# A decoder step's query and key passes: sample columns made once, TensorE in written order, rows fetched half a step ahead

## The chip, the cores and the metric

One core of one Trainium2 chip. The metric is the device time of one execution in microseconds, the median over several runs. One execution was also taken with the hardware profiler; all rows here are from it.

## The reference, cut to what matters

One step of a small decoder trunk: a state-space layer, then one shared key and value projection, then one attention layer. There are 2048 prompt rows and 8 sample rows (one new token for each of 8 sequences with 2048 cached positions), all 1024 wide. The part around the change projects the state-space layer's output x1 twice, each time after an RMS norm with its own scale and shift:

```
qz = (norm(x1) * (1 + scale_b)  + shift_b)  @ w_in_b     # 2048 + 8 rows -> queries q, gates z
kv = (norm(x1) * (1 + scale_kv) + shift_kv) @ w_kv       # 2048 + 8 rows -> keys k, values v
scores of a sample = q_sample . cached keys            # 16 pages of 128 keys, 16 heads
weights = stick-breaking(sigmoid(scores / 8 + bias))
```

Both norms divide by the same root mean square; only scale and shift differ, for the sample rows too. Keys and values of all rows are outputs.

## The kernel before, in words

The method `phase_b1` (L1085) makes both projections. Everything is float32; a product is three matmuls of reduced precision (`hi` by `hi`, `lo` by `hi`, `hi` by `lo`), so a weight `w` is kept as `w0h`, `w0l` (slot w0) or `w1h`, `w1l` (slot w1), and the normed columns as `hi`, `lo`.

**The loop** (L1190) has 16 steps, `(ps, t)`: pass 0 (queries and gates) for eight groups of 256 prompt rows, then pass 1 (keys and values) for the same eight. Group t = 1 carries the 8 sample rows beside its 256. A step of pass 0 (step 0 to 7) runs eight `q_block`s with slot w0 and eight `z_block`s with slot w1, 24 matmuls each. A step of pass 1 (step 8 to 15) runs eight `k_block`s, each followed by the two transposes (`k_rows`) of the key block before it, and two `v_block`s of 48 wide matmuls each (three for t = 1).

**The columns of the next step** are made within a step, in three parts. `norm_rows` (L1031) loads 256 rows of x1 as two tiles `x` (L1038; two buffers), has ACT take the sum of their squares (L1039), DVE a root by Newton steps (L90 to L95) and a scaling (L1043). The Square's discarded output `jk` needs a buffer of the pool tag "wraw" (three buffers), through which weight halves also stream (L890, L892, L893). `norm_cols` (L1053) is a generator: each of its eight pulls transposes 128 columns on PE into PSUM (`psC`), keeps a copy in DRAM for the second pass (`xn`, L1070 and L1071), and makes `h` (L1073, ACT), `hi` (L1074, ACT) and `lo` (L1075, POOL or DVE). In pass 1, for t > 0, `norm_again` (L1046) loads the kept transposed columns `xn`, so there are no transposes. For t = 1 a ninth pull loads the sample rows `xs` (L1079) and calls `sample_cols` (L855): Square, root, scaling (L861), eight small transposes, four DVE operations (L868 to L871).

The rows are fetched after the first block of a step (f == 0); the generator is made after block 3 (pass 0) or block 2 (pass 1) and then pulled ahead of each later block: the prompt rows' transposes stand ahead of query blocks 4 to 7 and z blocks 0 to 3, the sample rows' ahead of z block 4 or of value block 1.

**The sample keys.** Beside this, `sample_keys` (L1263) loads cached key pages (`kp`, three buffers, on SP's queue), multiplies them with the sample's query (DVE, L1275) and reduces them to scores `zs` (DVE, L1276). When a sample's scores are there, `sample_weights` makes its weights in four stages: transposes of `zs`, then of `c`, a small matmul of `E`, and transposes of `sg`, with ACT and DVE work between them. `more` pulls this stream after each query, z and key block from step 2 on and four times ahead of each value block. By the text, the four stages of sample 7, the last, all stand ahead of value block 0 of step 14, and the first stage of sample 3 right behind the key blocks of step 8.

**What sets the order.** The framework's scheduler orders each engine's instructions by a simulation of its own; the text gives only priorities. `keep_in_program_order` pins an instruction behind the one written before it on its engine; `Ordered` and `OrderedCore` apply it to whole engines, and so far only the attention phase behind this one used them. The DMAs of this phase go through SP's queue.

Of the kernel before, what the change touches and what calls it, by code (L numbers as in the profile page):

```python
# [9 lines left out]
FR = mybir.dt.float32r  # L10
# [16 lines left out]
KT = 8  # L27
# [19 lines left out]
class Ordered:  # L47


    def __init__(self, tc, engine):  # L50
        self.tc, self.engine = tc, engine
# [8 lines left out]


class OrderedCore:
    def __init__(self, tc, nc):
        self.nc = nc
        for n in ("tensor", "vector", "scalar", "gpsimd"):
            setattr(self, n, Ordered(tc, getattr(nc, n)))

    def __getattr__(self, name):
# [3 lines left out]
class Kern:  # L72
# [643 lines left out]
    def phase_a1(self):  # L716
        nc, tc, I, cp = self.nc, self.tc, self.I, self.cp
        self.W = {}
        self.uV = self.scr("uV", [NG, 8, GC, CH])
        self.uS = self.scr("uS", [D, NS])  # L720
        self.zT = self.scr("zT", [D, NC1])
        self.ygT = self.scr("ygT", [D, NC1])
        self.x1 = self.scr("x1", [NC1, D])
        self.gD = self.scr("gD", [2, 9, D])
        with ExitStack() as c1:
            self.s5c = self.pool(c1, "s5c", side="right")
            self.dmask = self.s5c.tile([64, 16], FT, name="dmask")
            nc.vector.tensor_add(self.dmask, self.idf[:64, 0:16], self.idf[:64, 32:48])
            wp = self.pool(c1, "wp", side="right")
            ep = self.pool(c1, "ep", 2, side="right")  # L730
            slots = iter(self.slots("w0"))
            self.h = [[[self.wr["w0"].tile([128, 2, 512], FR, tag=next(slots), name=f"h{cb}{g}") for _ in range(4)]
                       for g in "hl"] for cb in range(2)]
            W = lambda slot: self.split_w(wp, I["w_in_a"], 2 * D, slot * 128, 128)
            with ExitStack() as c2:
                with ExitStack() as ce:
                    early = self.pool(ce, "early")
                    early2 = self.pool(ce, "early2")
                    xp = self.pool(c2, "xp", side="right")
                    sc, sh = self.mod_tiles("a", 2)  # L740
                    with ExitStack() as c3:
                        mp = self.pool(c3, "mwp", side="right")
                        self.silu_c(early)
                        self.vectors(early)
                        b, g = self.vo["b_mod_a"], self.vo["g_pre_a"]
                        for f in range(2):
                            self.mod_finish(self.mod_wide(mp, I["w_mod_a"], f * 512, 512, 4), sh, f * 4, 4, b, None, 0)
                            self.mod_finish(self.mod_wide(mp, I["w_mod_a"], D + f * 512, 512, 4), sc, f * 4, 4, b + 8, g, 1.0)
                            if f == 0:
                                xt = self.x_block(xp, xp, 0)  # L750
                                w = [W(0), W(1)]
                    xq = self.pool(c2, "xq", side="right")
                    self.h_block(xp, 0, xt, sc, sh, range(HS))
                    xt1 = self.x_block(xp, xq, 1)
                    self.h_block(xp, 0, xt, sc, sh, range(HS, KT))
                    self.h_block(xp, 1, xt1, sc, sh, range(HS))
                    xt2 = self.x_block(xp, xp, 2)
                    self.h_block(xp, 1, xt1, sc, sh, range(HS, KT))
                    self.s5_params(early, early2)
                h23 = self.pool(c1, "h23")  # L760
                self.h += [[h23.tile([128, KT, n], FR, name=f"h{cb}{g}") for g in "hl"] for cb, n in ((2, 512), (3, 520))]
                self.h_block(xp, 2, xt2, sc, sh, range(HS))
                xt3 = self.x_block(xp, xq, 3)
                self.h_block(xp, 2, xt2, sc, sh, range(HS, KT))
                self.h_block(xp, 3, xt3, sc, sh, range(KT))
                self.kpad_zero(xp)
                xs = xp.tile([128, D], FT, tag="x", name="xs", bufs=4)[:8]
                nc.sync.dma_start(xs, I["x_sample"].rearrange("a b d -> (a b) d"))
                self.sample_cols(xp, xs, sc, sh, self.h[3][0], self.h[3][1], slice(512, 520))
            with ExitStack() as c2:  # L770
                self.sp = self.pool(c2, "sp", side="right")
                self.linears(wp, ep, w)
            with ExitStack() as c2:
                self.s5_states(self.pool(c2, "st", side="right"))
            with ExitStack() as c2:
                self.linears_tail(wp, ep, self.pool(c2, "gm", side="right"))
# [75 lines left out]
        for _ in mods:  # L852
            pass

    def sample_cols(self, pool, xs, sc, sh, hhi, hlo, cols, extra=None):  # L855

        nc = self.nc
        ss = pool.tile([8, 1], FT, tag="sss", name="sss")
        nc.scalar.activation(self.rp.tile([128, D], BF, tag="wraw", name="jk")[:8], xs, AF.Square, accum_out=ss)
        rs = self.rsqrt(pool, ss, 8, 1, "rss")  # L860
        nc.vector.tensor_scalar(xs, xs, rs, None, OP.mult)  # L861
        p = self.psC()
        for k in range(KT):
            self.tr(p[:, k * 8:(k + 1) * 8], xs[:, k * 128:(k + 1) * 128])
        pv = p[:, :64].rearrange("p (k s) -> p k s", s=8)
        for s_, b_, hi, lo in ([(sc, sh, hhi, hlo)] + ([extra] if extra else [])):
            t = pool.tile([128, KT, 8], FT, tag="sct", name="sct")
            nc.vector.tensor_mul(t, pv, s_[:, :, 1:9])  # L868
            nc.vector.tensor_add(t, t, b_[:, :, 1:9])
            nc.vector.tensor_copy(hi[:, :, cols], t)  # L870
            nc.vector.tensor_sub(lo[:, :, cols], t, hi[:, :, cols].bitcast(FT))  # L871
# [181 lines left out]
    def norm_cols(self, t, xt, mods, keep=None, kept=False):  # L1053


        nc, xp, hp = self.nc, self.xp, self.hp
        sc, sh = mods
        hi, lo = (hp[t % 2].tile([128, KT, 264], FR, tag=f"{g}{t % 2}", name=f"{g}{t % 2}") for g in ("hi", "lo"))

        def go():  # L1060
            for k in range(KT):
                if kept:
                    p = xt[k // 4][:, k % 4]
                else:
                    p = self.psC()[:, :256]
                    for i in range(2):
                        self.tr(p[:, i * 128:i * 128 + 128], xt[i][:, k * 128:(k + 1) * 128])
                if keep:
                    o = keep.tile([128, 512], FT, tag="v", name="xn")[:, :256]
                    nc.scalar.activation(o, p, AF.Copy)  # L1070
                    nc.sync.dma_start(self.xnT[k * 128:k * 128 + 128, t * 256:t * 256 + 256], o)  # L1071
                h = xp.tile([128, 256], FT, tag="h", name="h", bufs=2)
                nc.scalar.activation(h, p, AF.Identity, scale=sc[:, k, 0:1], bias=sh[:, k, 0:1])  # L1073
                nc.scalar.activation(hi[:, k, :256], h, AF.Copy)  # L1074
                (nc.gpsimd if k % 2 or kept else nc.vector).tensor_sub(lo[:, k, :256], h, hi[:, k, :256].bitcast(FT))  # L1075
                yield
            if t == 1:
                xs = xp.tile([128, D], FT, tag="x", name="xs", bufs=2)[:8]
                nc.sync.dma_start(xs, self.x1[SEQ:NC1])  # L1079
                self.sample_cols(xp, xs, sc, sh, hi, lo, slice(256, 264))  # L1080

        n = 264 if t == 1 else 256
        return go(), hi[:, :, :n], lo[:, :, :n]

    def phase_b1(self):  # L1085
        nc, tc, I, O = self.nc, self.tc, self.I, self.O

        self.kT = self.scr("kT", [NH, 2 * HD, SEQ])
        self.qT = self.scr("qT", [NH // 2, HD, 4, SEQ])
# [3 lines left out]
        with ExitStack() as c:  # L1093
            hp1 = self.pool(c, "b1h1", side="right")
            op = self.pool(c, "b1o", 2, side="right")
            sp = self.pool(c, "b1s", side="right")
            self.hp[1] = hp1
            self.sample_setup()
            units = self.sample_keys(sp)
            def fm_block(f, n, h, w):  # L1100
# [83 lines left out]
            def more():  # L1184
                done[0] += 1
                while done[1] < total * done[0] // (13 * 16):
                    done[1] += 1
                    next(units, None)

            for s, (ps, t) in enumerate(steps):  # L1190
                n = 264 if t == 1 else 256
                nxt = steps[s + 1] if s + 1 < 16 else None
                cols = iter(())
                for f in range(KT):
                    next(cols, None)
                    (k_block if ps else q_block)(f, t, n, h)
                    if s > 1:
                        more()
                    if f == 0 and nxt:
                        xt = self.norm_again(nxt[1]) if nxt[0] and nxt[1] else self.norm_rows(nxt[1])  # L1200
                    if f == (2 if ps else 3) and nxt:
                        cols, *nh = self.norm_cols(nxt[1], xt, mods[nxt[0]], None if nxt[0] else op, nxt[0] and nxt[1])
                if late:
# [10 lines left out]
                if ps == 0:  # L1214
                    for f in range(KT):
                        next(cols, None)
                        z_block(f, t, n, h)
                        if s > 1:
                            more()
# [7 lines left out]
                        v_block(i, t, h)  # L1227
                for _ in cols:
                    pass
                if nxt:  # L1230
                    h = nh
                if (ps, t) == (0, 7):
                    self.load_w("w1", I["w_kv"], 2 * D, D)
            for _ in units:
                pass


    def sample_setup(self):
# [533 lines left out]
```

## Time and profile before

| | us |
|---|---|
| median of 3 runs | 3251.82 (3247.64 to 3253.74) |
| the profiled execution | 3257.83 |
| its span on the core | 3256.1 |
| the 16 steps of `phase_b1` in it | 1083.4 to 1986.3 |

The mean granted TensorE clock of the profiled execution is 0.96 of full speed. Times in rows count from the start of the span. In rows, PE is TensorE, PEld its weight loads, DVE VectorE, ACT ScalarE, POOL GpSimd, SP SyncE; "psA<-hi,w0h" is an instruction that writes psA from hi and w0h, and a bracket behind it gives the engine's idle time ahead of it and what ended that. A row of a stretch gives its bounds, its length, then each engine's busy time with its instructions (PE, PEld, DVE, ACT, POOL), the granted TensorE clock as a share of full speed, the busy share of the DMA engines, and GB/s.

### The profile page before, as it was taken

The page shows a single profiled execution, that of the slowest core. Times are in us where ns is not written, and L with a number is a line of the kernel's source. Part 1 is how long each engine was busy: PE and PEld are TensorE (multiplying, and loading weights), DVE is VectorE, ACT ScalarE, POOL GpSimd, SP SyncE. Part 2 cuts the span into 40 slices and gives each one's busy share as a digit, 9 for nine tenths or more (in the row PEclk, how much of TensorE's full clock was granted, in tenths as well). Part 3 has the DMA queues.
Part 4 walks back from the last instruction along what each step waited for, and adds up shares of the span by engine and source line. Part 5 has one row for each costly group of instructions (what it writes and reads, how often), then busy time and mean ns, then how long its engine had stood idle before and what let it go on. Part 6 is the DMA issues. An engine that isn't in the chain of part 4 may idle for free.

```text
span 3256.1 us, 57087 instructions
## 1 busy us (share of the span) xinstructions
PE 2954.8 (91%) x19352; PEld 2343.4 (72%) x19352; DVE 2343.6 (72%) x4219; ACT 1314.8 (40%) x2954; POOL 1010.8 (31%) x1273
## 2 busy tenths in 40 slices
PE   7899989999999899898699999878899989999998
PEld 3666767778888799898588886555566656666777
DVE  7799998354434555667656545888899999898864
ACT  3422222232222533234333324555566665555541
POOL 1234433000000100000101103545576666565640
PEclk8999999999999899999899999999999999999999
DMA  7433333565543556667666667878766632333234
GB/s 221 136 95 102 101 98 96 168 179 152 145 128 115 185 156 196 188 192 221 203 190 204 196 191 223 226 202 239 214 207 192 205 101 74 114 106 92 87 104 136
DMA packets 498726, 519.52 MB, mean 160 GB/s; under 512 B 57989, under 2 KB 385958, under 8 KB 498242
## 3 DMA queue, kind: packets, MB, share of 16 engines
q1 hardware_dynamic: 493586, 514.46, 54.1%
q8 instruction: 154, 2.52, 0.3%
q10 hardware_dynamic: 4560, 1.35, 0.2%
q14 instruction: 138, 1.13, 0.1%
q0 software_dynamic: 288, 0.06, 0.0%
HBM read 384.97 MB, written 130.75 MB: 158 GB/s over the span
## 4 chain that ended last, share of the span: by engine, by line
PE 38%; DVE 30%; DMA 14%; issue 6%; ACT 4%; SPq 3%; POOL 2%; DVEq 0%; ACTq 0%; POOLq 0%
PE psA L78 14%; DVE cc L57 9%; PE psB L78 6%; DMA kp<-in_cache_k 5%; PE psZ L57 5%; PE psA L57 4%; PE psC L57 4%; PE psO L57 3%; DVE s L57 3%; DVE kp L1275 2%; PE psC L78 1%; DMA Q<-qT 1%; DVE zs L1276 1%; DVE A L591 1%; SPq L1253 1%
## 5 line engine op out<-in xcount | busy, mean ns | idle before, releaser
L57 ACT ACTIVATE s<-psZ,sbias 128x512 f32<-128x512 f32 (+2 forms) x640 | 375.8, 647 | 258.3 <-issue 114.3
L57 POOL TENSOR_TENSOR s<-s,cc 128x384 f32<-128x384 f32 (+2 forms) x288 | 363.1, 1261 | 204.6 <-DVE cc L57 161.5
L57 POOL TENSOR_SCALAR cc<-s 128x1024 f32<-128x1024 f32 (+3 forms) x320 | 319.6, 999 | 294.6 <-ACT s L57 272.5
L57 ACT ACTIVATE wT<-psC 128x512 f32<-128x512 f32 (+3 forms) x640 | 311.5, 542 | 178.8 <-PE psC L57 177.3
L57 DVE TENSOR_TENSOR_SCAN cc<-cc,zero 128x512 f32<-128x512 f32 (+5 forms) x256 | 355.3, 1408 | 38.7 <-POOL cc L57 38.7
L57 PE MATMUL psZ<-X,Q 128*128 128x512 f32 (+2 forms) x1280 | 364.8, 405 | 17.8 <-DMA Q<-qT 16.9
L57 PE MATMUL psC<-idf,s 128*128 128x128 f32 x2176 | 311.9, 284 | 44.3 <-ACT wT L57 36.7
L57 PEld LDWEIGHTS psC<-idf,s 128*128 128x128 f32 x2176 | 251.7, 145 | 133.6 <-ACT wT L57 55.2
L1075 POOL TENSOR_TENSOR lo<-h,hi 128x256 fp32r<-128x256 f32 x92 | 79.4, 873 | 783.2 <-ACT hi L1074 673.9
L57 DVE TENSOR_TENSOR_SCAN cc<-cc,car,zero 128x1025 f32<-128x1025 f32 x128 | 299.8, 2342 | 31.1 <-POOL cc L57 31.1
L78 PE MATMUL psA<-hi,w0h 128*128 128x256 f32 (+1 forms) x1024 | 304.0, 297 | 10.8 <-ACT w0h L892 4.1
L1275 DVE TENSOR_TENSOR kp<-kp,qb 128x512 f32<-128x512 f32 x256 | 179.0, 703 | 185.2 <-DMA kp<-in_cache_k 160.0
L78 PE MATMUL psA<-hi,w0l 128*128 128x256 f32 (+1 forms) x1024 | 295.2, 288 | 1.8 <-DVE w0l L893 1.8
L78 PE MATMUL psA<-lo,w0h 128*128 128x256 f32 (+1 forms) x1024 | 295.0, 288 | 0.2 <-DVE lo L871 0.2
L57 DVE TENSOR_TENSOR s<-s,cc 128x640 f32<-128x640 f32 (+2 forms) x320 | 274.7, 858 | 24.2 <-ACT wT L57 0.9
L57 PEld LDWEIGHTS psZ<-X,Q 128*128 128x128 f32 x1280 | 214.5, 195 | 77.3 <-issue 39.0
L57 PE MATMUL psO<-wT,V 128*64 128x256 f32 (+1 forms) x2304 | 258.4, 373 | 5.9 <-DVE zb L57 5.8
L57 PEld LDWEIGHTS psO<-wT,V 128*64 128x64 f32 x2304 | 158.5, 137 | 92.2 <-issue 15.7
L78 PEld LDWEIGHTS psA<-hi,w0h 128*128 128x128 f32 x1024 | 201.5, 197 | 13.0 <-DVE z L1127 4.6
L78 PEld LDWEIGHTS psA<-hi,w0l 128*128 128x128 f32 x1024 | 200.5, 196 | 2.5 <-DVE w0l L893 2.5
L78 PEld LDWEIGHTS psA<-lo,w0h 128*128 128x128 f32 x1024 | 201.2, 196 | 0.8 <-POOL lo L1075 0.5
L1276 DVE TENSOR_REDUCE zs<-kp 128x8 f32<-128x512 f32 x256 | 174.0, 683 | 5.6
(413 smaller groups left out, 6736.2 us busy)
## 6 DMA issues: line engine op xcount, KB each, us to landing
kp<-in_cache_k SPq DMA_DIRECT2D x256, 256.0 KB
vp<-in_cache_v SPq DMA_DIRECT2D x256, 256.0 KB
Q<-qT SPq DMA_DIRECT2D x128, 256.0 KB
x<-x SPq DMA_DIRECT2D x50, 512.0 KB
X<-kT SPq DMA_DIRECT2D x48, 512.0 KB
x<-in_x_prompt SPq DMA_DIRECT2D x32, 512.0 KB
qT<-kq SPq DMA_DIRECT2D x128, 128.0 KB
kT<-kq SPq DMA_DIRECT2D x128, 128.0 KB
```

What stands on the lines that cost most here:

```text
L57: return self.tc.keep_in_program_order(f(*a, **k))
L78: self.nc.tensor.matmul(out, lhsT, rhs, start=start, stop=stop, skip_group_check=True)
L591: V.tensor_tensor_scan(sg[:, ri], r8, d[:, ri], 0.0, OP.mult, OP.add)
L1075: (nc.gpsimd if k % 2 or kept else nc.vector).tensor_sub(lo[:, k, :256], h, hi[:, k, :256].bitcast(FT))
L1253: ld, (r,) = nc.values_load_multi_w_load_instructions(self.pt[:, s * NPG + pg:s * NPG + pg + 1], engines=[mybir.EngineType.SP], min_val=0, ...
L1275: nc.vector.tensor_mul(kp, kp, qb)
L1276: nc.vector.tensor_reduce(zs[:, pg, a * 8:a * 8 + 8], kp.rearrange("p (h d) -> p h d", h=8), axis=mybir.AxisListType.X, op=OP.add)
```

## The change

`sample_cols` takes any number of targets; the columns of the sample rows for pass 1 are made together with those for pass 0, in step 0, into two new tiles `skv`, and copied in place in step 8 with two DVE copies. `phase_b1` runs with an `OrderedCore` for TensorE alone. The rows of step 1 are fetched ahead of the loop (behind the load of slot w1); those of step s + 2 ahead of z block 6 of step s in pass 0, once the generator is drained, and at the end of step s in pass 1.

```diff
 class OrderedCore:
-    def __init__(self, tc, nc):
+    def __init__(self, tc, nc, names=("tensor", "vector", "scalar", "gpsimd")):
         self.nc = nc
-        for n in ("tensor", "vector", "scalar", "gpsimd"):
+        for n in names:
             setattr(self, n, Ordered(tc, getattr(nc, n)))
...
-    def sample_cols(self, pool, xs, sc, sh, hhi, hlo, cols, extra=None):
+    def sample_cols(self, pool, xs, *dsts):
...
-        for s_, b_, hi, lo in ([(sc, sh, hhi, hlo)] + ([extra] if extra else [])):
+        for s_, b_, hi, lo, cols in dsts:
...
-            if t == 1:
+            if t == 1 and kept:
+                for d, p in ((hi, self.skv[0]), (lo, self.skv[1])):
+                    nc.vector.tensor_copy(d[:, :, 256:264], p)
+            elif t == 1:
                 xs = xp.tile([128, D], FT, tag="x", name="xs", bufs=2)[:8]
                 nc.sync.dma_start(xs, self.x1[SEQ:NC1])
-                self.sample_cols(xp, xs, sc, sh, hi, lo, slice(256, 264))
+
+                self.sample_cols(xp, xs, (sc, sh, hi, lo, slice(256, 264)), (*self.mkv, *self.skv, slice(0, 8)))
...
     def phase_b1(self):
-        nc, tc, I, O = self.nc, self.tc, self.I, self.O
+        plain = self.nc
+        nc = self.nc = OrderedCore(self.tc, plain, ("tensor",))
+        tc, I, O = self.tc, self.I, self.O
...
+            self.skv = [hp1.tile([128, KT, 8], FR, name=f"skv{g}") for g in "hl"]
...
+            fetch = lambda ps, t: self.norm_again(t) if ps and t else self.norm_rows(t)
+            xt = fetch(*steps[1])
             for s, (ps, t) in enumerate(steps):
...
-                    if f == 0 and nxt:
-                        xt = self.norm_again(nxt[1]) if nxt[0] and nxt[1] else self.norm_rows(nxt[1])
...
                     for f in range(KT):
                         next(cols, None)
+                        if f == 6 and s < 14:
+                            for _ in cols:
+                                pass
+                            xt = fetch(*steps[s + 2])
                         z_block(f, t, n, h)
...
                 for _ in cols:
                     pass
+                if ps and s < 14:
+                    xt = fetch(*steps[s + 2])
...
+        self.nc = plain
```

## Rows read from the trace of the kernel before

**Rows 1.** The page: PE's busy time, and the chain that ended last by engine.
```profile
PE 2954.8 (91%) x19352; PEld 2343.4 (72%) x19352; DVE 2343.6 (72%) x4219; ACT 1314.8 (40%) x2954; POOL 1010.8 (31%) x1273
...
PE 38%; DVE 30%; DMA 14%; issue 6%; ACT 4%; SPq 3%; POOL 2%; DVEq 0%; ACTq 0%; POOLq 0%
```

**Rows 2.** Busy time by stretch: steps 0, 2, 6, 7, 8, 14, 15; sum of all 16.
```profile
1083.40:1150.40 67.00, 53.80 (x410) 52.02 (x408) 34.70 (x93) 34.13 (x77) 5.17 (x6) 0.87 0.65 198
...
1199.50:1246.70 47.20, 47.20 (x402) 47.20 (x401) 29.34 (x55) 16.82 (x43) 3.89 (x4) 1.00 0.70 199
...
1411.30:1464.80 53.50, 49.56 (x407) 49.16 (x406) 32.79 (x73) 17.89 (x46) 3.50 (x4) 0.97 0.69 192
1464.80:1520.60 55.80, 50.37 (x411) 49.43 (x410) 44.33 (x94) 22.30 (x51) 3.71 (x4) 0.97 0.76 223
1520.60:1610.40 89.80, 52.62 (x319) 45.76 (x317) 61.36 (x111) 32.63 (x74) 8.54 (x10) 0.84 0.71 214
...
1884.00:1939.50 55.50, 50.95 (x315) 45.49 (x314) 28.40 (x51) 18.21 (x46) 6.92 (x9) 0.94 0.64 188
1939.50:1986.30 46.80, 46.80 (x306) 42.36 (x305) 3.41 (x8) 10.07 (x29) 0.00 (x0) 1.00 0.87 245
sum 902.90, PE 810.27 PEld 754.57 DVE 526.16 ACT 308.37 POOL 77.51; mean PE 50.64 PEld 47.16 DVE 32.88 ACT 19.27 POOL 4.84
```

**Rows 3.** Waits from 1080 to 1986: waiting operation, releaser, total us, times, longest.
```profile
DVE kp L1275 <- DMA kp<-in_cache_k: 160.0, 132, 5.3
...
ACT kq L1117 <- DMA qT<-kq: 70.1, 26, 10.3
...
ACT jk L1039 <- DMA x<-x: 32.8, 11, 7.1
...
PE psC L83 <- DVE xs L861: 24.7, 2, 24.6
...
PE psC L83 <- ACT kf L1145: 20.4, 9, 4.5
...
PE psC L83 <- DVE x L1043: 14.2, 4, 5.3
```

**Rows 4.** Timeline of step 0: start, us, engine, line, operation, [idle before it].
```profile
1084.24 0.42 SPq L1038 DMA_DIRECT2D x<-x  x1
...
1103.53 0.28 PE L78 MATMUL psA<-lo,w0h 128*128 128x256 f32 x1
...
1119.38 1.06 ACT L1039 ACTIVATE jk<-x 128x1024 bf16<-128x1024 f32 x1
...
1125.47 0.90 PE L83 MATMUL psC<-idf,x 128*128 128x128 f32 x3 [4.98 <-DVE x L1043]
...
1135.73 0.38 PE L83 MATMUL psC<-idf,x 128*128 128x128 f32 x2
...
1144.08 0.63 PE L83 MATMUL psC<-idf,xs 8*128 8x8 f32 x8 [0.17 <-DVE xs L861]
...
1144.75 0.23 DVE L868 TENSOR_TENSOR sct<-psC,mod_b 128x64 f32<-128x64 f32 x1 [0.81 <-PE psC L83]
```

**Rows 5.** Timeline of step 8: sample 3's last reduce, the sample rows' transposes.
```profile
1577.14 0.69 DVE L1276 TENSOR_REDUCE zs<-kp 128x8 f32<-128x512 f32 x1
...
1608.02 0.99 PE L83 MATMUL psC<-idf,xs 8*128 8x8 f32 x8 [24.56 <-DVE xs L861]
```

**Rows 6.** Timeline of step 14: last key transposes, sample 7's last reduce and last stage.
```profile
1915.05 0.38 PE L83 MATMUL psC<-idf,kf 128*128 128x128 f32 x2
...
1927.51 0.69 DVE L1276 TENSOR_REDUCE zs<-kp 128x8 f32<-128x512 f32 x1
...
1935.12 0.38 PE L83 MATMUL psC<-idf,sg 128*128 128x128 f32 x2
```

**Rows 7.** Timeline of steps 7 and 14: PE's longest waits for late rows.
```profile
1482.12 1.05 PE L83 MATMUL psC<-idf,x 128*128 128x128 f32 x2 [5.27 <-DVE x L1043]
...
1903.49 0.69 PE L83 MATMUL psC<-idf,kf 128*128 128x128 f32 x2 [4.50 <-ACT kf L1145]
```

More of the change, by code (lines that the diff above doesn't have):

```diff
@@ L768, in phase_a1 @@
                 nc.sync.dma_start(xs, I["x_sample"].rearrange("a b d -> (a b) d"))
-                self.sample_cols(xp, xs, sc, sh, self.h[3][0], self.h[3][1], slice(512, 520))
+                self.sample_cols(xp, xs, (sc, sh, self.h[3][0], self.h[3][1], slice(512, 520)))
             with ExitStack() as c2:
```

## The prediction

> **What bounds the kernel now.** I read the page first: TensorE is busy for 91% of the span, yet the chain that ended last runs through it for only 38% and through DVE for 30% [rows 1]. An average over phases says little here, so I cut the query and key passes into their 16 steps. In [rows 2] the reader should compare step 2, where PE is busy for all of 47.2 us at full clock, with the others: step 15 takes 46.8, but step 0 takes 67.0, step 8 takes 89.8 at a mean clock of 0.84, step 14 takes 55.5. All 16 together have 810.27 us of PE work in 902.90 us. So PE is the bound, and what a change can win or lose is PE's gaps, 93 us of them, and the clock that falls behind them. The list of waits says who makes the gaps [rows 3]: DVE's scaled sample rows (24.7 us, nearly all in one wait), the keys' copies on ACT (20.4 in 9), the scaled prompt rows (14.2 in 4). ACT and DVE wait far more (70.1 us for the stores of the query tiles, 160.0 for cache pages), which costs PE only where one of its operands hangs on it.
>
> Prices I use: a block of 24 matmuls is 47.2 / 16 = 2.95 us, the transposes of its step included; the two value blocks of a step are 46.8 less eight key blocks at some 3.06 (with their two transposes), 22.3 us. Steps 6 and 7 have a granted clock of 0.97 [rows 2], 3% of 53.5 and 55.8, so a gap of a few us costs about 1.65 us more in slow matmuls behind it.
>
> **The change, part by part.**
>
> *Written order on PE.* The scheduler had let PE run what was ready. It departs from the order of the text in few places, three of them of size.
>
> (a) Step 0, prompt rows. Their transposes are written ahead of query block 4. The rows are asked for at 1084.24, but the Square needs a scratch tile of the pool through which the second weight half of this layer streams; it runs at 1119.38, behind nearly all of the weight's pieces, and the first transpose at 1125.47. PE was through query block 3 at about 1103.7 and filled the time with five blocks [rows 4]. The fetch moves ahead of the loop but stays behind the weight's load, so the scratch tile comes no sooner. In written order the five blocks (5 x 2.95 = 14.7 us) run after the wait, plus 1.65 of slow clock: at most +16.3. With no query stores of those blocks on SP's queue and no evictions on ACT the weight may stream a few us faster; at best the Square is ready early and this costs 0. The rows speak for the upper half: I take +12 (0 to +16.3).
>
> (b) Step 0, sample rows. Their transposes are written ahead of z block 4. The last prompt transposes start at 1135.73, the sample's at 1144.08 [rows 4]: 8.0 us after the former end, in which PE ran other z blocks. Only z block 3 (2.95) stays ahead: 5.0 of wait and 1.65 of clock, +6.7 (0 to +8). The second set of columns, made here, is four DVE operations on 64 columns like the 0.23 us one in [rows 4], about 0.9 us on an engine with 34.70 of 67.0 us busy; nobody waits for them before step 9, so nothing. If that cover went, 0.9.
>
> (c) Step 8. The key pass's sample columns become two DVE copies; with them go a transfer, a Square, a root, a scaling and eight transposes. These transposes waited 24.56 us for the scaled rows [rows 5]; with the slow clock behind it the wait is worth 26.2. But the scheduler had run the value blocks ahead. In written order the transposes of sample 3's scores stand right behind key block 7, ahead of both value blocks, and their last reduce starts at 1577.14, ending near 1577.8 [rows 5]. Both value blocks follow: 1577.8 + 0.3 + 22.3 + 2 for a cold start is 1602.4, where step 8 ended at 1610.4: -8 (-26.2 if the reduce comes early, 0 if it comes as late again as the wait now does).
>
> (d) Step 14. Here all four stages of sample 7 are written ahead of value block 0. Now PE ends key block 7 at about 1915.2 and runs the value blocks at once; the last reduce starts at 1927.51, the last stage's transposes at 1935.12 [rows 6]. In order, the value blocks begin at 1935.5 and end 22.3 later, 1957.8, for 1939.5: +18.3. Should the reduces be ready at key block 7's end, the chain of stages alone (1928.2 to 1935.5, less about 1 us of PE work that is in the step anyway) costs +6.4. I take +18.3, since the pages come at the pace of SP and DVE, which no edit touches. Queued behind these waits is all of PE; the value copies on ACT and their stores wait with it.
>
> *Fetch half a step ahead.* (e) Of the 14.2 us for scaled rows, 4.98 are step 0's [rows 3, 4]; 9.2 are in steps 6 and 7, the longest 5.27 [rows 7]. Rows asked for ahead of the last step's z block 6 have six blocks (18 us) in place of three. The clock of both steps gives 3.3 more: -12.5. It is 0 if the rows are late for another reason, and at most -33, if also every wait of ACT for rows (32.8) reached PE [rows 3]. On SP's queue the two transfers move ahead of the stores of two z blocks and one query block and of the pages between; their tiles are free by then (the transposes are drained first), so they hold nobody up. Their Squares (1.06 us each on ACT [rows 4]) and root on DVE move along and are not added to; the z blocks' evictions that they may delay have PSUM buffers to wait in, so nothing for that, at worst those 2 us in a step.
>
> (f) In the key pass, the transposed rows are asked for one key block sooner only. The key copy that made PE wait 4.50 us [rows 7] stands on ACT behind the next step's columns, which wait for these rows. One block of 2.95 helps some of the 9 waits: -5 of 20.4 (-18 at best). The transfers now wait on SP for tiles that ACT and POOL free with the last columns, and the pages queue behind them; +4.5, the wait of [rows 7] once more, bounds that.
>
> (g) The remaining reorderings (a few value matmuls ahead of the last key transposes in each of eight steps; the sample queries in step 1) are below 1 us each: +5 (0 to +8).
>
> Sum: 12 + 6.7 - 8 + 18.3 - 12.5 - 5 + 5 = **+16.5**. The profiled execution took 3257.83 us, 6.0 above the median of 3251.82, so 3274.3 on its own basis and 3268 for the median. The terms' bounds, not all at one end at once, make it +2 to +28.
>
> **A rule that speaks for another end.** Each late row of (e) leaves the same gap on PE, ahead of query block 4. The Trainium skill, "Perfetto Trace Analysis", section Optimization Strategy, says that the same gap repeating on the engine that should be saturated can mean that no SBUF or PSUM is free for the next tile. By it, asking sooner would win nothing and (e) would be 0; the trace bears it out in so far as ACT waits 70.1 us for two query tiles to be stored [rows 3]. It is the second rival below.
>
> **The rivals.**
>
> Faster: the scores keep pace with PE. One mechanism: the page loads are written between PE's blocks and SP takes them in order, so if PE loses its gaps in steps 4 to 8, the reduces of samples 3 and 7 come earlier by as much. They decide where they are ready at key block 7's end, some 16 us sooner in step 8 and 12 in step 14. Then (c) is -26.2 and (d) +6.4: 12 + 6.7 - 26.2 + 6.4 - 12.5 - 5 + 5 = -13.6, 3238 us. For it: DVE waits 160.0 us for pages, so it is not itself full [rows 3]. Against it: that same wait means the stream is late wherever PE is.
>
> Slower still: earlier rows win nothing, because Square and the next steps' columns sit on ACT, in order, behind evictions that wait for query stores. (e) and (f) go: +34, 3286. For it: 70.1 us of such waits. Against it: step 7's rows came from a late request rather than a full queue [rows 7].
>
> No change: half of the faster rival's lead, (c) -17 and (d) +12.4: +1.6, 3253.
>
> The change doesn't do what it says: written order alters nothing where it matters (other engines' new schedule already has the scores ready). (a), (b), (d) and (g) are 0: -26.2 - 12.5 - 5 = -43.7, 3208. Against it: the present trace departs from written order at all three places.
>
> **How the numbers follow.** Forecast 0.36, faster rival 0.26, halfway case 0.16, slower still 0.15, inert order 0.07. A measurement here can tell about 0.2%, 6.5 us. Faster: 0.26 + 0.07 = 0.33. Same: 0.16 and 0.04 of the forecast's low end, 0.20. Slower: 0.32 + 0.15 = 0.47. The range runs from 3228, below the faster rival, to 3290, above the slower one, and leaves out the inert case and the outer parts of both, under 0.2. As both signs are likely, the forecast's own range: 3254 to 3280.
>
> **What would show it.** Step 0 at 80 us or more, with one PE gap of about 20 us ahead of the prompt's transposes: (a). A step 8 near 82 whose gap now stands ahead of the value blocks: (c). Step 14 near 73 with a gap of some 13 us behind key block 7: (d). Steps 6 and 7 near 48: (e). I am wrong if step 0 stays at 67, or if the scores' transposes in steps 8 and 14 come without a wait.

## The result, and the profile after

The change makes the kernel slower: 3290.97 us (median of 4 runs, 3286.62 to 3298.25) for 3251.92 (4 runs), a ratio of 1.0132 with a 95% interval of 1.0114 to 1.0149. The forecast had the side right (3268, +16.5) and the size wrong: +39 lies 1 us beyond the range of all its cases (3228 to 3290) and 11 beyond the forecast's own (3254 to 3280).

First the page of the changed kernel, busy time and the chain that ended last:

```profile
PE 2968.3 (90%) x19344; PEld 2356.9 (71%) x19344; DVE 2340.9 (71%) x4209; ACT 1313.7 (40%) x2952; POOL 1005.5 (31%) x1273
...
PE 20%; DVE 17%; DMA 8%; issue 4%; SPq 3%; ACT 2%; POOL 1%; DVEq 0%; ACTq 0%; POOLq 0%
```

The work is the same as in [rows 1], eight transposes and ten DVE instructions fewer; the span is 40 us longer. So PE stands still for longer. The stretches say where: steps 0, 4, 5, 6, 7, 8, 9, 11, 13, 14 of the changed kernel, columns as in [rows 2].

```profile
1084.63:1171.49 86.86, 56.01 (x410) 54.41 (x408) 37.59 (x106) 35.30 (x76) 5.49 (x6) 0.80 0.49 152
...
1319.11:1374.93 55.82, 50.98 (x408) 50.46 (x409) 37.73 (x85) 18.90 (x49) 3.71 (x4) 0.94 0.69 199
1374.93:1427.63 52.70, 50.19 (x411) 49.67 (x409) 35.72 (x77) 17.60 (x46) 3.54 (x4) 0.97 0.68 196
1427.63:1478.12 50.49, 47.83 (x407) 47.52 (x405) 34.88 (x75) 15.50 (x42) 3.42 (x4) 1.00 0.69 200
1478.12:1537.41 59.29, 51.41 (x410) 50.40 (x409) 41.54 (x91) 22.84 (x52) 3.28 (x4) 0.94 0.69 202
1537.41:1619.88 82.47, 53.24 (x311) 46.49 (x309) 55.54 (x95) 28.73 (x66) 6.35 (x8) 0.83 0.73 222
1619.88:1690.40 70.52, 63.65 (x370) 49.52 (x368) 41.13 (x76) 21.44 (x53) 6.83 (x8) 0.95 0.65 197
...
1740.33:1798.32 57.99, 50.16 (x310) 44.85 (x309) 34.83 (x58) 17.09 (x45) 5.79 (x8) 0.94 0.66 194
...
1846.54:1906.38 59.84, 53.94 (x315) 47.52 (x314) 37.05 (x65) 17.36 (x46) 6.28 (x8) 0.91 0.67 195
1906.38:1978.17 71.79, 52.63 (x316) 46.08 (x315) 26.94 (x46) 18.02 (x46) 6.63 (x9) 0.83 0.47 138
```

Beside [rows 2]: step 0 +19.9, step 6 -3.0, step 7 +3.5, step 8 -7.3, step 14 +16.3. Of the others, steps 4 and 5 are 2.7 and 3.0 shorter than before, steps 9, 11 and 13 are 5.4, 4.4 and 4.9 longer. These three were, in the kernel before:

```profile
1610.40:1675.50 65.10, 62.98 (x369) 50.86 (x370) 39.56 (x73) 18.59 (x47) 5.96 (x7) 0.96 0.65 192
...
1724.40:1778.00 53.60, 49.16 (x309) 44.19 (x308) 32.96 (x57) 17.20 (x45) 6.12 (x8) 0.97 0.67 198
...
1829.10:1884.00 54.90, 50.35 (x316) 45.04 (x315) 31.82 (x60) 17.64 (x46) 6.19 (x8) 0.97 0.69 198
```

The next table sums this up for the main kernels of this study. PE's waits in the 16 steps, against [rows 3]; `zs` are the scores, `kf` the key copies, `x` and `xs` the scaled prompt and sample rows, `h` the column copies:

```profile
PE psC L57 <- DVE zs L1290: 34.4, 5, 13.2
PE psC L57 <- ACT kf L1152: 25.7, 15, 8.3
PE psC L57 <- DVE x L1043: 20.4, 2, 20.2
PE psC L57 <- ACT h L1073: 12.8, 6, 4.5
PE psC L57 <- DVE xs L861: 4.4, 1, 4.4
```

Two of these in the kernel before, which [rows 3] does not show:

```profile
PE psC L83 <- ACT h L1073: 7.9, 4, 4.1
...
PE psC L83 <- DVE zs L1276: 0.4, 1, 0.4
```

(All of PE's instructions of this phase now have line 57, that of the ordering helper; kernel lines behind the change are shifted by 5 to 14.) The sample rows' 24.7 us have shrunk to 4.4, the one wait left in step 0. New at the top are the scores: 34.4 us in five waits, for 0.4 before. The timeline of the changed kernel shows the wait of step 0 and three of these five, with the reduces that end the longest two:

```profile
1119.77 1.06 ACT L1039 ACTIVATE jk<-x 128x1024 bf16<-128x1024 f32 x1
...
1125.45 0.48 PE L57 MATMUL psC<-idf,x 128*128 128x128 f32 x1 [20.24 <-DVE x L1043]
...
1593.40 0.69 DVE L1290 TENSOR_REDUCE zs<-kp 128x8 f32<-128x512 f32 x1
1594.14 0.47 PE L57 MATMUL psC<-idf,zs 128*128 128x128 f32 x1 [9.61 <-DVE zs L1290]
...
1769.92 0.48 PE L57 MATMUL psC<-idf,zs 128*128 128x128 f32 x1 [5.27 <-DVE zs L1290]
...
1945.67 0.69 DVE L1290 TENSOR_REDUCE zs<-kp 128x8 f32<-128x512 f32 x1
1946.41 0.48 PE L57 MATMUL psC<-idf,zs 128*128 128x128 f32 x1 [13.15 <-DVE zs L1290]
```

Step 0 is as forecast: the Square at 1119.77, for 1119.38 in [rows 4], and a PE that may not run ahead. Sample 3 holds step 8 for 9.61 us and sample 7 step 14 for 13.15, as forecast. Sample 5 in step 11 (5.27), and samples 4 and 6 in steps 9 and 13 (4.45 and 1.94), were not.

### The profile page after: what moved, and what is told of

It is laid out like the page before. It is cut to its first block, busy times and chain, and to the rows that moved or that the text cites. A ratio compares the mean times of both kernels' runs of the same rounds, so it can differ in the third digit from the quotient of the medians.

```text
span 3296.5 us, 57053 instructions
## 1 busy us (share of the span) xinstructions
PE 2968.3 (90%) x19344; PEld 2356.9 (71%) x19344; DVE 2340.9 (71%) x4209; ACT 1313.7 (40%) x2952; POOL 1005.5 (31%) x1273
## 3 DMA queue, kind: packets, MB, share of 16 engines
q1 hardware_dynamic: 493570, 514.43, 53.1%
## 4 chain that ended last, share of the span: by engine, by line
PE 20%; DVE 17%; DMA 8%; issue 4%; SPq 3%; ACT 2%; POOL 1%; DVEq 0%; ACTq 0%; POOLq 0%
DVE cc L57 9%; PE psA L57 8%; PE psZ L57 5%; PE psC L57 4%; DMA kp<-in_cache_k 3%; PE psO L57 3%; DVE s L57 3%; DMA Q<-qT 1%; DVE kp L1289 1%; DVE y L57 1%; DMA vp<-in_cache_v 1%; SPq L1267 1%; DVE zs L1290 1%; DMA wraw<-in_w_kv 1%; ACT s L57 1%
## 5 line engine op out<-in xcount | busy, mean ns | idle before, releaser
L57 ACT ACTIVATE s<-psZ,sbias 128x512 f32<-128x512 f32 (+2 forms) x640 | 375.6, 646 | 264.5 <-issue 126.5
L57 PE MATMUL psZ<-X,Q 128*128 128x512 f32 (+2 forms) x1280 | 367.4, 407 | 21.2 <-DMA Q<-qT 20.2
L57 PEld LDWEIGHTS psO<-wT,V 128*64 128x64 f32 x2304 | 158.8, 138 | 88.4 <-issue 15.6
```

The costliest lines, as they stand in the source:

```text
L57: return self.tc.keep_in_program_order(f(*a, **k))
```

## The experiments

Step lengths run from the first matmul of a step's first block to that of the next. Each kernel here is made from the changed one, if nothing else is said. Times are medians in us; in each group the kernel before ran on the same chip, at 3252 to 3253. The steps of a row come from one profiled execution, which lay between 10 us below and 9 us above its kernel's median, so a few us between two rows say little.

| kernel | median | step 0 | steps 1-7 | step 8 | steps 9-15 |
|---|---|---|---|---|---|
| before | 3251.92 | 67.0 | 370.2 | 89.8 | 376.0 |
| the change | 3290.97 | 86.9 | 365.9 | 82.5 | 405.6 |
| e1 no order | 3251.92 | 67.7 | 373.2 | 62.0 | 400.4 |
| e2 order only | 3283.93 | 87.0 | 374.1 | 100.8 | 375.6 |
| e3 no fetch | 3291.43 | 88.2 | 373.6 | 83.9 | 402.9 |
| e4 late scores | 3274.28 | 88.4 | 369.8 | 73.9 | 393.1 |
| e8 late scores, rows first | 3262.88 | 69.7 | 370.1 | 73.8 | 389.8 |
| e13 no order, stores by ACT | 3225.66 | 67.8 | 372.2 | 66.3 | 382.2 |
| e17 before, stores by ACT | 3249.28 | 67.9 | 369.2 | 87.7 | 379.2 |
| e18 columns alone, stores by ACT | 3227.00 | 67.1 | 366.4 | 62.4 | 380.9 |

### Which part costs: e1 to e3

e1 leaves out the written order, e2 is the kernel before with the order alone, e3 leaves out the earlier fetch.

```diff
e1, in phase_b1:
-        plain = self.nc
-        nc = self.nc = OrderedCore(self.tc, plain, ("tensor",))
-        tc, I, O = self.tc, self.I, self.O
+        nc, tc, I, O = self.nc, self.tc, self.I, self.O
...
-        self.nc = plain
e3, in the loop:
+                    if f == 0 and nxt:
+                        xt = fetch(*nxt)
...
-                        if f == 6 and s < 14:
-                            for _ in cols:
-                                pass
-                            xt = fetch(*steps[s + 2])
e2: both edits of the columns and of e3 undone, the order kept
```

> The change without the written order (columns and fetch stay). Order theory (PE is held by late operands only because it may not pass them): the long waits of step 0 and for sample scores go, the columns' gain of some 25 us and the fetch's 9 stay: 3215 to 3230. Fetch theory (the earlier requests crowd SP and ACT, so that key copies and scores come late by themselves): 3250 to 3275. Neither, if it stands near 3291.

> The kernel before with the written order alone (no kept columns, fetch as before). Order theory: the change's +39, and in step 8 the wait of some 24 us for the sample rows, now ahead of value block 1 with nothing to fill it; and the rows' waits in steps 4 to 6 come back (9): 3300 to 3325. Fetch theory: under 3270.

> The change without the earlier fetch (order and columns stay). Order theory: steps 4 to 6 lose the 9 us that they gained, everything else stays: 3291 to 3303. Fetch theory: the waits for key copies in step 8 (8.3 and 7.1) and those for scores in steps 9, 11 and 13 go: 3260 to 3280.

Measured: e1 0.9993 (0.9975 to 1.0011), e2 1.0094 (1.0057 to 1.0132), e3 1.0108 (1.0070 to 1.0147). The order is what costs: alone (e2) it adds 31 us, and without it (e1) the kernel is level with the one before. e2 lies between its two ranges, 16 us below the order theory's, because step 8 is 18 us longer than in the change (24 expected) but steps 9 to 15 are 30 us shorter, step 14 alone by 11. In e2 the last scores of sample 7 are ready some 10 us before PE comes to their transposes:

```profile
1926.38 0.69 DVE L1281 TENSOR_REDUCE zs<-kp 128x8 f32<-128x512 f32 x1
...
1937.49 0.64 PE L57 MATMUL psC<-idf,zs 128*128 128x128 f32 x2
```

With the columns kept (e3, the change) PE waits there for over 13 us. So sample 7 is late when the order meets a shorter step 8, and not by the order alone. The fetch does nothing either way (e3 is the change to within 0.5 us), so the fetch theory falls although e1's number lay in its range. But the order theory is wrong about e1 too: kept columns and earlier rows ought to have gained 25 us and more, and they gain nothing. The table has the reason in one line: step 8 falls from 89.8 to 62.0, 27.8 us as (c)'s upper bound had it, and steps 9 to 15 grow from 376.0 to 400.4, 24.4 us. The time is handed back. The same in written order: from e2 to e3 step 8 loses 16.9 us and steps 9 to 15 gain 27.3, and the medians' intervals overlap.

### Who takes it back: e5, e6 and e7

In e5 (no order) and e6 (order) `more` pulls nothing, so all remaining pages of the sample keys follow step 15. The scheduler still brought the first two samples' pages forward into steps 1 to 5; from step 6 on there are none.

```diff
             def more():
-                done[0] += 1
+                return
```

> The change without the written order, and no page of the sample keys is pulled within the 16 steps: all 256 follow behind step 15 (the time of the run is longer by that and says nothing; its steps do). Page theory (from step 8 on a step lasts as long as its share of pages takes, so time freed in step 8 is handed back in steps 9 to 15): steps 8 to 15 last 47 to 51 us each, some 400 together, for 462 in the change without order. Rival (the steps wait for their own stores and key copies): 440 or more.

> The same with the written order (again only the steps count). Page theory with late scores: without scores to wait for, the order costs step 0's 20 us and little else: steps 1 to 15 together within 10 us of the run without order. Rival (the order costs PE by key copies and column copies too): 20 us or more in steps 1 to 15.

Each ran once. The stretch of e1's step 10 and the sum of its steps 8 to 15:

```profile
1649.62:1707.52 57.90, 51.07 (x314) 44.95 (x313) 36.08 (x65) 19.01 (x47) 6.44 (x8) 0.94 0.64 189
...
sum 462.39, PE 415.15 PEld 359.70 DVE 254.61 ACT 151.93 POOL 45.03; mean PE 51.89 PEld 44.96 DVE 31.83 ACT 18.99 POOL 5.63
```

The same of e5:

```profile
1615.06:1661.85 46.79, 46.79 (x306) 42.35 (x304) 3.91 (x8) 16.63 (x45) 5.82 (x8) 1.00 0.40 102
...
sum 397.67, PE 390.10 PEld 347.06 DVE 45.74 ACT 137.12 POOL 40.89; mean PE 48.76 PEld 43.38 DVE 5.72 ACT 17.14 POOL 5.11
```

Without pages, steps 10 to 15 are 46.8 us of PE each, at full clock, and steps 8 to 15 last 397.67 for 462.39. So it is this stream that lengthens the steps: the pages, and the samples' weights made from them. The pages do not need that long by themselves: behind step 15 of e5, 192 of them take 336 us, 1.75 us each; in steps 9 to 14 of e1, 126 take 348 us, 2.8 us each. And the sums of steps 1 to 15, first of e5, then of e6:

```profile
sum 746.84, PE 726.80 PEld 679.88 DVE 212.63 ACT 263.58 POOL 62.41; mean PE 726.80 PEld 679.88 DVE 212.63 ACT 263.58 POOL 62.41
```

```profile
sum 746.37, PE 727.89 PEld 680.53 DVE 209.75 ACT 264.54 POOL 63.04; mean PE 727.89 PEld 680.53 DVE 209.75 ACT 264.54 POOL 63.04
```

Without pages the written order costs nothing outside step 0 (there 87.5 for 67.7). All that it costs later it costs together with the stream of pages.

e7 is e1 with `13 * 16` replaced by `14 * 16 + 4` in `more`, which spreads the stream over the pulls of all steps.

> The change without the written order, the pages spread over 228 pulls in place of 208. Page theory: each step has a tenth less of the stream to carry, 3225 to 3243. Rival: 3246 to 3258, as without the edit.

3244.14 (0.9970, 0.9959 to 0.9980) falls between the two. The 16 steps lost 28.5 us (874.70 for 903.2 in e1), but the phase behind them, 1271 us in e1, lasted 1288: the stream's end now reaches into it.

### The waits of the order: e4 and e8

e4 writes the four stages of a sample's weights later, those of sample 7 into step 15; e8 also asks for step 1's rows ahead of the load of the second weight half.

```diff
e4, in sample_keys:
-                    if (a * NPG + pg) % 6 == 2:
+                    if (a * NPG + pg) in (8, 14, 20, 26):
...
+        for _ in range(14):
+            yield
         for _ in chain:
e8, besides, in phase_b1:
+            fetch = lambda ps, t: self.norm_again(t) if ps and t else self.norm_rows(t)
+            xt = fetch(*steps[1])
             self.load_w("w1", I["w_in_b"], 2 * D, D)
...
-            fetch = lambda ps, t: self.norm_again(t) if ps and t else self.norm_rows(t)
-            xt = fetch(*steps[1])
```

> The change with the stages of each sample's weights written six pulls later (sample 7's fourteen). Order theory, with the scores as the main cause: the 34 us of waits for reduces and some slow clock behind them go: 3248 to 3265. Rival (the wait only moves on to the next late operand, the key copies): above 3280.

> The change with the late scores of the run before, and step 1's rows asked for ahead of the load of the second weight half, so that their Squares have a scratch tile early. If step 0's 20 us are the Square's wait for that pool: 3274 less 15 to 20, 3253 to 3262. If the rows are late for another reason: 3270 to 3280.

e4: 3274.28, between its two ranges: 17 us less than the change, where the order theory expected 26 to 43. Two of PE's waits in e4:

```profile
PE psC L57 <- ACT kf L1152: 35.3, 20, 8.5
...
PE psC L57 <- DVE zs L1290: 1.0, 1, 1.0
```

The waits for scores are gone, 34.4 to 1.0; those for key copies grew from 25.7 to 35.3. Half of the rival holds: some of the wait moves on to the next operand that is late. e8: 3262.88, another 11 less, just above its range. Step 0 of e8, and the Square that sets it:

```profile
1078.28:1148.00 69.72, 56.60 (x410) 54.58 (x409) 37.30 (x106) 34.99 (x77) 5.45 (x6) 0.85 0.62 191
```

```profile
1086.59 1.06 ACT L1039 ACTIVATE jk<-x 128x1024 bf16<-128x1024 f32 x1 [0.49 <-DVE w0l L893]
```

The Square runs at 1086.59 in place of 1119.77 and step 0 is back at 69.7 us, 18.6 less than in e4 (the median falls by 11 only; e8's profiled execution was the fastest of its six). SP asks for the rows among the same pieces of the weight in both kernels, and the 0.49 us ahead of the Square end with `w0l`, the last reader of a buffer of that pool. Term (a)'s cause, a scratch tile behind the weight's pieces, is shown.

### Through which queue: e9 to e18

e9 gives every second page one of the weight pool's three buffers (`self.rp`, tag "wraw"), so that six pages can be under way, without the order; e10 is the same with it, e11 the same on the kernel before, e12 on e8.

```diff
-                    kp = sp.tile([128, 512], FT, tag="kp", name="kp", bufs=3)
+                    kp = sp.tile([128, 512], FT, tag="kp", name="kp", bufs=3) if pg % 2 else \
+                        self.rp.tile([128, 512], FT, tag="wraw", name="kp")
```

> The change without the written order; every second page goes to the three buffers of the weight pool, so six pages can be under way in place of three. Page theory, with the buffers as what sets the pace: pages come at 2.2 us or less each in steps 10 to 14 in place of 2.5 to 3, those steps last 48 to 52 and the run 3215 to 3238. Rival (the pace is SP's, DVE's or the DMA engines', not the buffers'): 3243 to 3260.

> The change itself with the six page buffers. Page theory: the waits for scores in steps 9, 11 and 13 go and those in 8 and 14 shrink, step 0 stays at 87: 3255 to 3275. Rival (buffers do not set the pace): 3284 to 3300.

> The kernel before with the six page buffers. Page theory: steps 9 to 14 near 48 to 51, step 8 still with its 24 us for the sample rows: 3230 to 3245. Rival: 3243 to 3260.

> The change with step 1's rows ahead of the weight, the late scores and the six page buffers. Page theory: no large wait of the order is left, 3215 to 3240, near the same without order. Rival: 3255 to 3268, as without the buffers.

Measured: e9 3233.06 (0.9923, 0.9899 to 0.9947), as the page theory had it; e10 3297.36 and 40.2 us of waits for scores, as the rival had it; e11 3247.57 (0.9986, 0.9972 to 0.9999), hardly a gain, in the rival's range; e12 3251.44 (0.9990, 0.9977 to 1.0003), between its ranges. So six buffers give 19 us with the columns and no order (e9 for e1), little without the columns (e11), nothing in the change itself (e10), and 11 us in written order once scores and rows are mended (e12 for e8). Buffers are not the whole pace. What stands between the pages and PE shows in e1 from step 9 on: SP's two largest waits, for the data of a key store (`kT`, L1117) and for a page's buffer (L1271), then ACT's largest waits for stores. (`kq` is a key tile's two halves, `pk` a tile of key rows, `v` one of values; `pk` and `v` share two buffers.)

```profile
SPq L1117 <- DVE kq L1153: 26.5, 12, 3.6
SPq L1271 <- DVE zs L1287: 26.4, 36, 2.5
```

```profile
ACT pk L1142 <- DMA out_p_v<-v: 37.5, 10, 8.3
ACT kq L1152 <- DMA kT<-kq: 35.4, 16, 4.4
ACT v L1167 <- DMA out_p_v<-v: 22.3, 12, 5.6
```

A stretch of e1's step 10 shows how they stand on SP:

```profile
1676.01 0.36 SPq L1271 DMA_DIRECT2D kp<-in_cache_k  x1
1680.82 1.24 SPq L1117 DMA_DIRECT2D kT<-kq  x2
1682.11 0.60 SPq L1143 DMA_DIRECT2D out_p_k<-pk  x1
1683.49 0.36 SPq L1271 DMA_DIRECT2D kp<-in_cache_k  x1
```

The key stores wait for their data (3.6 us, for `kq`), and the next page comes behind them. The other way round, a page that waits for a buffer (until DVE has reduced an older one) holds the key and value stores behind it; ACT waits for the tiles of these stores; and PE, it seemed, waits for ACT's key copies. e13 takes key-row and value stores off SP, without the order; e14 adds the six buffers; e15 is the change itself with these stores moved, e16 is e12 with them.

```diff
-                nc.sync.dma_start(dram(O["p_k"], t * 256 * D + f * 128, [[D, 128], [128 * D, 2], [1, 128]]), pk)
+                nc.scalar.dma_start(dram(O["p_k"], t * 256 * D + f * 128, [[D, 128], [128 * D, 2], [1, 128]]), pk)
...
-                    nc.sync.dma_start(dst, v)
+                    nc.scalar.dma_start(dst, v)
```

> The change without the written order; the stores of key rows and of values are issued by ACT, which makes them, in place of SP. SP theory (stores stand behind pages that wait for a buffer, evictions behind the stores, PE behind the evictions): steps 9 to 15 lose half of their excess of 65 us over the run without pages, 3215 to 3235. Pace theory (the pages themselves take that long): 3245 to 3258.

> Both remedies without the order: stores by ACT and six page buffers. SP theory: a little under either alone, 3205 to 3230. Pace theory: 3228 to 3238, as with six buffers alone.

> The change itself with these stores issued by ACT. If the order's loss is late scores and step 0: waits for key copies shrink, those for scores stay, 3275 to 3292. If SP's queue makes the scores late as well: 3245 to 3270.

> The order with every remedy (step 1's rows first, late scores, six buffers, stores by ACT). SP theory: 3215 to 3240. Pace theory: 3245 to 3258, as without the stores' move (3251).

e13: 3225.66 (0.9920, 0.9896 to 0.9945); e14: 3217.29 (0.9881, 0.9848 to 0.9915), the fastest kernel here, 34 us below the one before. Both are in the SP theory's range, though steps 9 to 15 of e13 lose 18 us of their 60 over e5 and not half. The stream runs ahead: its last reduce ends 8.9 us into step 14 of e13, and 9.2 us into step 15 of e1. The last link is not shown, though: in steps 9 to 15 PE's waits for key copies hardly change (23.7 us in e1, 21.2 in e13). What falls is the wait for key rows `pk` (6.4 us, then none) and PE's busy time (364.3 to 357.1), at a granted clock of 0.98 for 0.96. e15: 3271.78 (1.0069, 1.0047 to 1.0091), 19 under the change, between its two ranges and 2 us above that of "SP makes the scores late as well". Its waits of PE:

```profile
PE psC L57 <- ACT kf L1152: 32.0, 15, 7.2
...
PE psC L57 <- DVE zs L1290: 11.2, 1, 11.2
```

Of five waits for scores one is left, in step 8; step 14 lasts 56.8 for 71.8. Six buffers had left 40.2 us of such waits (e10), so it is the stores on SP that make most of the scores late. e16: 3247.81 (0.9989, 0.9971 to 1.0006), in the range of the pace theory and 8 us above that of the SP theory: with every remedy the written order is level with the kernel before, and still 30 us above e14, which has both remedies for SP and no order.

The last two separate the parts with SP relieved: e17 is the kernel before with the stores by ACT, e18 has the kept columns besides, with rows fetched as before and no order.

> The kernel before with key-row and value stores issued by ACT: neither kept columns nor earlier rows. If the freed queue lets the columns' gain stay, this run lacks it: 3240 to 3254, for 3225.66 with both. If the time in step 8 was never worth anything: 3220 to 3234.

> The same with the kept columns, rows fetched as before. If the earlier fetch gains nothing: 3220 to 3234, as with both. If it is the fetch that gains: 3236 to 3252.

Moved stores alone: 3249.28 (0.9991, 0.9976 to 1.0005), nothing clear of the noise. With the kept columns: 3227.00 (0.9915, 0.9896 to 0.9933), as much as with the fetch too (e13). Both lie in their first range. (Columns alone with the stores on SP did not run; e1, which has the fetch too, stands for them.) ACT's waits for value stores, 37.5 and 22.3 us in e1, are no longer among its larger ones in e18, though those for key stores grew from 35.4 to 53.1. Step 8's gain stays: 62.4, and 380.9 in steps 9 to 15.

One rival is untested. From step 9 on, DVE's largest wait in e1 is not for pages (41.3 us) but for the half of a key tile that ACT makes, and the pages' products share DVE with it:

```profile
DVE kq L1153 <- ACT kq L1152: 91.9, 40, 7.5
```

It is 62.9 us in e13. No run takes this work off DVE, so how much of the pages' pace is DVE's queue and not SP's is open.

## Why the prediction was wrong, by its own steps

**(a), (b): right.** Step 0 grew by 19.9 us, +18.7 forecast, through the gaps that were named: 20.24 ahead of the prompt's transposes, 4.4 for the sample rows (5.0 forecast). Their slow clock added 2.2 us of busy time (3.3 forecast). The cause named in (a) is shown by e8.

**(c): right.** Step 8 lost 7.3 us, -8 forecast; its gap stands ahead of the value blocks, and sample 3's last reduce ends 56.7 us into the step, for 57.2 before. The "2 for a cold start" stands on no row; behind that wait the two value blocks took 25.2 us for 22.3.

**(d): right.** Step 14 grew by 16.3 us, +18.3 forecast, with 13.15 of wait for sample 7's reduce. By e2 this holds only because (c) held too.

**(e): wrong.** "The clock of both steps gives 3.3 more: -12.5": steps 6 and 7 together changed by +0.5. The waits for scaled rows did go (20.4 us in two waits, of which step 0's is 20.2), but those for the column copies `h` grew from 7.9 to 12.8 us, and step 7 has a wait of 4.53 us for such a copy, where it had one of 5.27 us for scaled rows. With the order off or on, the fetch is worth nothing in the medians (e13 for e18, the change for e3); in steps 1 to 7 it is 7.7 us of gain with the order and 5.8 of loss without, each from one execution.

**(f) and (g): wrong by as much.** (g) read "the remaining reorderings (a few value matmuls ahead of the last key transposes in each of eight steps; the sample queries in step 1) are below 1 us each: +5", and with (f)'s -5 they cancelled. Steps 9 to 13 grew by some 13 us (5.4, 1.0, 4.4, -2.9, 4.9), with three waits for scores of 4.45, 5.27 and 1.94 us. In the kernel before PE's order happened to be the written one at these places, so I took the order there to be free. But a place in the order is free only while the operand keeps its lead. The two transposes of sample 4's scores in step 9, first before and then in the change:

```profile
1664.19 0.38 PE L83 MATMUL psC<-idf,zs 128*128 128x128 f32 x2
```

```profile
1671.83 0.27 PE L57 MATMUL psC<-idf,zs 128*128 128x128 f32 x1
1676.56 0.48 PE L57 MATMUL psC<-idf,zs 128*128 128x128 f32 x1 [4.45 <-DVE zs L1290]
```

PE now reaches them 52.0 us into the step, 1.8 sooner than before; the last reduce ends 56.6 us in, 4.9 later than before.

Summed over the profiled executions, with the forecast behind each: step 0 +19.9 (+18.7), steps 1 to 7 -4.3 (-12.5), step 8 -7.3 (-8), steps 9 to 13 and 15 +13.4 (0), step 14 +16.3 (+18.3); together some +38 (+16.5).

The error behind these steps is one: I treated the gaps of PE as independent and added them. From step 2 on each step also carries its pages, and what PE saves in one place it waits for in another. (c), (e) and (f) booked 25.5 us of gains; (c)'s share came out as forecast in step 8 itself and was given back behind it. The runs show it: the order alone costs 31 us (e2), and columns and fetch on top of it gain nothing (the change is 7 us slower, the intervals overlapping); without the order they gain nothing either (e1); and without the stream steps 1 to 15 take the same time with and without the order (e5, e6). The rival "slower still" came close in its number (3286), but its reason, ACT's evictions that wait for query stores, is untested: ACT waits 69.3 us for them in the change, for 70.1 before, and no run moved them. The stores that e13 to e18 moved were those of key rows and values, and with them it was the columns' gain that came back. Why (e) came to nothing stays open. The faster rival fell on its one condition: in the change PE comes to sample 7's transposes at 1932.93 and the reduce ends 13 us later, so the stream did not keep pace. The rule of the Trainium skill on repeating gaps ("Perfetto Trace Analysis", Optimization Strategy), by which (e) would be 0, pointed in the right direction, with a limit: more page buffers were worth 19 us without the order (e9 for e1), nothing in the change itself (e10), and moving the stores, which adds no buffer, was worth more (26 us, e13 for e1).

What stays open besides: why sample 3's scores still come 11.2 us late with the stores moved, what the order still costs in e16, and what holds steps 10 to 14 of e13 and e14 at 48 to 58 us where 46.8 would do; ACT's largest wait for a store is there for the key stores that SP still issues, but no run moved those.

## What to carry to other kernels

Before adding up gaps of the busiest engine, ask what else each stage has to bring through: take that stream out once and look at the stages bare. A wait that is removed pays only if the queue behind the next wait is free, so a change that gains nothing may need a second one (here columns with the fetch 0, stores alone 3 and within the noise, columns and stores 25 us). Outside step 0 a fixed order on one engine cost nothing here where the steps ran bare, and was dear with a small side stream beside them. Writing that stream's work well behind its data gave back only a part (17 us, e4), and with every remedy the order still cost 30 us (e16 for e14).

## What the runs showed of the hardware

Behind a long gap PE starts at a low granted clock. In step 0 of the change, behind the 20.24 us in which it stood still:

```profile
1125.40:1128.40 3.00, 2.76 (x12) 2.47 (x13) 1.05 (x2) 1.26 (x3) 0.00 (x0) 0.50 0.13 44
1128.40:1131.40 3.00, 3.00 (x24) 3.00 (x24) 0.32 (x2) 0.71 (x3) 0.00 (x0) 0.86 0.00 0
1131.40:1134.40 3.00, 3.00 (x28) 3.00 (x27) 0.36 (x2) 1.47 (x5) 0.73 (x1) 1.00 0.53 131
```

It is 0.50, the lower of its two levels, in the first 3 us, and full speed again in the third 3 us. The 0.80 of the whole step is a mean that has the gap itself in it. A wait on PE therefore costs more than its length, as the forecast had allowed for: the same 410 matmuls of step 0 are 56.01 us of busy time in the change and 53.80 before.

Issuing twelve stores or more in each step of the second pass from ACT in place of SP costs nothing that can be measured (e17: 0.9991, 0.9976 to 1.0005).
